# Gathering the half-array products of a hybrid decoder layer into common slots

## The chip, the cores and the metric

The kernel runs on one core of one Trainium2 chip. The metric is the device time of one execution in microseconds; before the change three runs took 1182.36 to 1182.70 us, median 1182.63.

## The reference

Two layers run one after the other on 256 tokens of width 1024, all in float32. Each layer is a mixer and a squared-ReLU MLP, with a layer norm after each. The mixer has one input projection and two branches: attention with 16 heads of 64 (the block of 256 tokens is the whole sequence, so it is plain causal attention), and a state-space branch with 32 heads of 64 in 8 groups, whose chunk is the whole sequence too.

```python
q, k, v, z, xbc, dt_raw, g_att, g_ssm = split(x @ w_in)
att   = softmax(causal(rope(q) @ rope(k).T / 8)) @ v                 # 16 heads
xs, bm, cm = split(silu(causal_conv(xbc)))
decay = exp(a_cs[l] - a_cs[s]) for s <= l                            # a_cs: running sum of dt * a
y     = (cm @ bm.T * decay * dt) @ xs + d_skip * xs                  # 32 heads, 8 groups
y     = rmsnorm(y * silu(z)) * ssm_norm_w
mix   = (sigmoid(g_att) * (att @ w_attn_proj) + sigmoid(g_ssm) * (y @ w_ssm_proj)) @ w_out
h     = LN(ALPHA * x + mix);  x = LN(ALPHA * h + relu(h @ w_up)**2 @ w_down)
```

## The kernel before

The kernel writes its order out by hand. The program is a row of slots of TensorE, 370 a layer; a slot is twelve products of 256 columns or six of 512. `plan_layer` hangs work on slot numbers: `slots[s]` holds the slot's own products of the large projections, and `at(s, step)` hangs any other step on a slot. The last loop of `trunk` goes through the slots and issues for each the weight splits that are due (`high_half`, L121, a cast on ACT; `low_half`, L129, a subtraction on DVE), then the steps in the order in which they were hung, then the weight loads (L115, SP's queue), then the slot's own products. Every engine works through its instructions in that order. `res(s)` returns the next slot that no other step has reserved for a temporary PSUM bank.

Every large product is made of three float32r products (high by high, high by low, low by high parts; L139 to L141 where 512 columns are streamed, L402 to L404 where 256 are). Weights are loaded in half units of 512 KB, eight slots before the cast, which is two slots before the subtraction, which is four slots before use.

Between the large products stand small ones in plain float32. For attention, a pair of heads p takes: `at_scores` (L631; rows of 64, one head in each half of the array, so 64x128; both temporary banks), `at_mask` on DVE (L639), `at_exp` on ACT (L646), `at_norm` on DVE (L651, L653), one `at_turn` a head (three transposes, L660, and a copy on ACT, L662), `at_av` (L674; 64 output columns a head, one head in each half of the array, so 128x64), and for every second p `at_out`. For the state space, a pair of heads p takes: `ss_load` (a broadcast DMA on SP's queue into `pb`), `ss_seg` on DVE (L720), `ss_exp` on ACT (L726), `ss_mask` on DVE (L734) and `ss_y` (L745, also 128x64). For every second p, g = p // 2, follow `ss_sum`, the gate, the squares and `ss_mean` (L784, a full-array float32 product), then the scaling and splitting. `at_av` and `ss_y` write to the two banks of tag `yav`.

Before, the scores of pair p start at the first free slot from AT0[p], which gives 95, 108, 115, 130, 137, 146, 155 and 166; the two `at_turn` follow from four slots after the first exponential, and `at_av` comes four slots after the second `at_turn`. `ss_y` of p comes at int(72 + 6.75 p) + 6. In slots 74 to 113 the large products are those of q, k and v with 512 columns; from 114 those of z and the gates with 256.

Of the kernel before, what the change touches and what calls it, by code (L numbers as in the profile page):

```python
# [11 lines left out]
F32 = mybir.dt.float32  # L12
# [6 lines left out]
S = 256  # L19
# [17 lines left out]
START = -10  # L37
AT0 = (95, 108, 109, 130, 134, 146, 155, 166)
SS0, SS_STRIDE = 72, 6.75


# [19 lines left out]
def trunk(ctx: ExitStack, tc: tile.TileContext, x, xT, pos, w, pch, hp, lnp, out):  # L61
# [7 lines left out]

    # The program is a row of slots of the tensor engine (about 6 products of 512 columns each).  # L70
    # Every slot first issues the weight loads and splits due in it, then the steps hung on it,
    # then its own products.
    slots = {}
    steps = defaultdict(list)
# [10 lines left out]
    def res(s):  # L85
        """the next slot in which nothing takes a bank for turning data."""
        s = int(s)
        while s in busy:
            s += 1
        busy.add(s)  # L90
        return s
# [12 lines left out]

# [1 line left out]
    raws = {}  # L106
# [35 lines left out]

# [1 line left out]
    def cols(base, L, h0, src, alloc, nk=KD, outer_from=None, quiet=False):  # L144
# [37 lines left out]

# [1 line left out]
    def rows(base, L, h0, k0, accs, src, outer=False):  # L184
# [24 lines left out]

# [1 line left out]
    ident = consts.tile([128, 128], F32, name="ident")  # L211
# [18 lines left out]

# [1 line left out]
    x_tok = consts.tile([128, 2, D], F32, name="x_tok")  # L232
# [22 lines left out]

# [1 line left out]
    cos2 = consts.tile([128, 2, 16], F32, name="cos2")  # L257
# [48 lines left out]

# [1 line left out]
    def new_T(name):  # L308
        return (u_tile(name + "h", F32R, (128, 4, S)), u_tile(name + "l", F32R, (128, 4, S)))

    def transpose_half(s, dst, src, t, j, name):
        """four 128-column blocks of one token tile."""
        tp = new_tmp(name).rearrange("p (k s) -> p k s", k=4)
        for k in range(4):
            nc.tensor.transpose(tp[:, k, :], src[:, k * 128:k * 128 + 128], ident)
        split_psum(s, dst[0][:, j:j + 4, t * 128:t * 128 + 128], dst[1][:, j:j + 4, t * 128:t * 128 + 128], tp)

    def transpose_pair(src, c, name):
        """two 128-column blocks of both token tiles."""
        tp = new_tmp(name).rearrange("p (k s) -> p k s", k=2)  # L320
        for k in range(2):
            for t in range(2):
                nc.tensor.transpose(tp[:, k, t * 128:t * 128 + 128],
                                    src[:, t, c + k * 128:c + k * 128 + 128], ident)
        return tp
# [3 lines left out]

# [1 line left out]
    class Norm:  # L331
# [47 lines left out]
    def plan_layer(L):  # L379
# [9 lines left out]

        at(B - 40 if L else START, load_params)  # L390
        xsrc = lambda k: (X[2 * L][0], X[2 * L][1], k)

        def gemm_ct(o, h, half, src=None, k0=None, nh=1):
            """a tile of 128 output columns, channel-major; four k-tiles of a half unit."""
            wh, wl = W[L, h]
            src = src or xsrc
            k0 = 4 * half if k0 is None else k0
            for i in range(4):
                k, c = k0 + i, (4 * half + i) * 128
                xh, xl, kk = src(k)  # L400
                a, b = wh[:, c:c + 128], wl[:, c:c + 128]
                nc.tensor.matmul(o, a, xh[:, kk, :], start=(k == 0), stop=False)  # L402
                nc.tensor.matmul(o, a, xl[:, kk, :], start=False, stop=False)  # L403
                nc.tensor.matmul(o, b, xh[:, kk, :], start=False, stop=(k == 8 * nh - 1))  # L404

# [1 line left out]
        def dt_slot(half):  # L407
# [72 lines left out]

# [1 line left out]
        XB = B + 10  # L482
# [56 lines left out]

# [1 line left out]
        T = {}  # L541
# [45 lines left out]

# [1 line left out]
        def ct_bank(base, h0, c0, c1, name, src, nh=1):  # L589
            """tiles c0..c1 of 128 output columns side by side in one bank."""  # L590
            g = {}

            def slot(c, half):
                if c == c0 and half == 0:
                    g["o"] = new_acc(f"acc_{name}{L}_{c}")
                o = g["o"][:, (c - c0) * S:(c - c0) * S + S]
                gemm_ct(o, h0 + nh * c + half // 2, half % 2, src, 4 * half, nh)

            for c in range(c0, c1):
                for half in range(2 * nh):  # L600
                    s = base + 2 * nh * c + half
                    if half % 2 == 0:
                        need(L, h0 + nh * c + half // 2, s)
                    slots[s] = (slot, c, half)
            return g

# [1 line left out]
        zs, ga, gs = {}, {}, {}  # L608
# [11 lines left out]

# [1 line left out]
        G = {}  # L622
# [61 lines left out]

        for p in range(8):
            s = B + AT0[p]
            while s in busy or s + 1 in busy:
                s += 1
            busy.update((s, s + 1))
            at(s, at_scores, p)  # L690
            for h in (2 * p, 2 * p + 1):
                at(s + 1, at_exp, h)
                at(s + 2, at_norm, h)
                s += 1
            s += 3
            for h in (2 * p, 2 * p + 1):
                s = res(s)
                at(s, at_turn, h)
                s += 1
            at(s + 3, at_av, p)  # L700
            if p % 2 == 1:
                at(s + 4, at_out, s + 4, p // 2)

# [1 line left out]
        E = {}  # L705
        yT = {}

        def ss_load(p):
            E["pb", p] = sb.tile([128, 2, S], F32, name=f"pb{L}_{p}", tag="pb", bufs=3)
            nc.sync.dma_start(out=E["pb", p].rearrange("p i s -> p (i s)"),  # L710
                              in_=P["csd"][2 * p:2 * p + 2, :].rearrange("h s -> (h s)").partition_broadcast(128))

        def ss_seg(p):
            pb = E.pop(("pb", p))
            e = sb.tile([128, 2, 384], F32, name=f"ev{L}_{p}", tag="e3", bufs=2)
            cst = P["cst"]
# [63 lines left out]
        def ss_mean(g):  # L780
            tp = new_tmp(f"sqp{L}{g}")
            sh = E.pop(("sh", g))
            for j in range(2):
                nc.tensor.matmul(tp[:, 0:S], ones, sh[:, j, :], start=(j == 0), stop=(j == 1))  # L784
            # every row of the product holds the sums; blocks of 32 columns turn them onto partitions
            r = sb.tile([128, S], F32, name=f"rs{L}{g}", tag="rs", bufs=1)
# [30 lines left out]
        free = 0  # L817
        for p in range(16):
            s = int(B + SS0 + SS_STRIDE * p)
            at(s - 12, ss_load, p)  # L820
            at(s - 1, ss_seg, p)
            at(s + 2, ss_exp, p)
            at(s + 3, ss_mask, p)
            at(s + 6, ss_y, p)
            if p % 2 == 1:
                g = p // 2
                at(s + 7, ss_sum, g)
                s = free = max(s + 8, B + 114 + 8 * (g // 2) + 10, free + 7)
                for i, step in ((-1, ss_gate), (1, ss_square), (2, ss_add), (3, ss_sq_high), (5, ss_sq_low)):
                    at(s + i, step, g)  # L830
                s = res(s + 8)
                at(s, ss_mean, g)
                at(s + 2, ss_rstd, g)
                at(s + 2, ss_scale, g)
                at(s + 3, ss_high, g)
                at(s + 5, ss_low, g)

# [1 line left out]
        mT, mb = {}, {}  # L839
# [30 lines left out]

# [1 line left out]
        at(B + 202, load_ln, gb1, L, 0)  # L872
# [23 lines left out]

# [1 line left out]
        M = B + 242  # L898
# [23 lines left out]

        # the other chunks channel-major: no turning needed
        ub = {}
# [116 lines left out]
def _cols(m, c0, n):  # L1041
    """n*512 columns -> for each 512, K/256 halves [128, 2 k, 512]."""
    kb = m.shape[0] // 256
# [4 lines left out]
def _rows(m):  # L1048
    """[K, 1024] -> K/128 halves [128, 1024]."""
    return m.reshape(-1, 128, D)  # L1050


def _tiles(m, starts):
    """tiles of 128 columns -> for each, K/1024 halves [128, 8 k, 128]."""
    out = [m[:, a:a + 128].reshape(-1, KD, 128, 128).transpose(0, 2, 1, 3).reshape(-1, 128, HALF) for a in starts]
    return np.concatenate(out)
# [62 lines left out]
```

## Time and profile before

| | |
|---|---|
| three runs | 1182.36 to 1182.70 us, median 1182.63 |
| span of the profiled execution, first to last instruction | 1179.1 us |
| PE (matmul) busy | 1160.1 us, 98% |
| PEld (weight load) busy | 1058.6 us, 90% |
| DVE busy | 865.3 us, 73% |
| ACT busy | 649.2 us, 55% |
| POOL busy | 51.1 us, 4% |
| chain that ended last | PE 96%, DVE 2%, DMA 1% |

The profile is that of one execution, and shows its span; the time of a run is counted around it and is some 3.5 us more. PE's matmuls are pipelined, so their durations overlap and the distance from one start to the next is what an instruction costs. The shapes after MATMUL are the rows and columns of the array that an instruction uses: 128*128 is the whole array.

### The profile page before, as it was taken

The page shows a single profiled execution, that of the slowest core. Times are in us where ns is not written, and L with a number is a line of the kernel's source. Part 1 is how long each engine was busy: PE and PEld are TensorE (multiplying, and loading weights), DVE is VectorE, ACT ScalarE, POOL GpSimd, SP SyncE. Part 2 cuts the span into 40 slices and gives each one's busy share as a digit, 9 for nine tenths or more (in the row PEclk, how much of TensorE's full clock was granted, in tenths as well). Part 3 has the DMA queues.
Part 4 walks back from the last instruction along what each step waited for, and adds up shares of the span by engine and source line. Part 5 has one row for each costly group of instructions (what it writes and reads, how often), then busy time and mean ns, then how long its engine had stood idle before and what let it go on. Part 6 is the DMA issues. An engine that isn't in the chain of part 4 may idle for free.

```text
span 1179.1 us, 20423 instructions
## 1 busy us (share of the span) xinstructions
PE 1160.1 (98%) x8160; PEld 1058.6 (90%) x8160; DVE 865.3 (73%) x1553; ACT 649.2 (55%) x927; POOL 51.1 (4%) x67
## 2 busy tenths in 40 slices
PE   6999999999999999999999999999999999999996
PEld 5999878999999889989889997789999998998995
DVE  4988977789866874564688888678997668556455
ACT  5665655788734363453456656568785343444341
POOL 1000000011110000000000000000110100000000
PEclk9999999999999999999999999999999999999999
DMA  9545554444466755556325455445534666555630
GB/s 348 193 143 180 188 176 150 166 144 144 147 208 218 249 183 187 190 201 246 133 99 216 158 191 187 162 143 171 161 134 172 220 218 207 204 179 183 210 125 36
DMA packets 61262, 211.37 MB, mean 179 GB/s; under 512 B 6992, under 2 KB 7344, under 8 KB 61168
## 3 DMA queue, kind: packets, MB, share of 16 engines
q1 hardware_dynamic: 59136, 204.04, 49.8%
q0 software_dynamic: 1744, 5.51, 1.5%
q8 instruction: 64, 1.05, 0.3%
q10 hardware_dynamic: 288, 0.52, 0.1%
q14 instruction: 30, 0.25, 0.1%
HBM read 208.93 MB, written 1.11 MB: 178 GB/s over the span
## 4 chain that ended last, share of the span: by engine, by line
PE 96%; DVE 2%; DMA 1%; SPq 0%; POOL 0%; issue 0%; POOLq 0%; ACT 0%
PE acc_x L402 5%; PE acc_x L403 5%; PE acc_x L404 5%; PE acc_d L140 5%; PE acc_d L139 5%; PE acc_d L141 5%; PE up L404 5%; PE up L403 5%; PE up L402 5%; PE acc_z L402 3%; PE acc_sp L403 3%; PE acc_sp L402 3%; PE acc_sp L404 3%; PE acc_z L403 3%; PE acc_z L404 3%; PE yp L745 2%
## 5 line engine op out<-in xcount | busy, mean ns | idle before, releaser
L129 DVE TENSOR_TENSOR wlo<-raw,whi 128x1024 fp32r<-128x1024 f32 (+1 forms) x371 | 443.7, 1216 | 28.7 <-ACT whi L121 12.7
L121 ACT CAST whi<-raw 128x1024 fp32r<-128x1024 f32 (+1 forms) x371 | 375.7, 1043 | 28.5 <-PE acc_ap L403 7.6
L500 DVE SCALAR_TENSOR_TENSOR cv<-acc_x,pc,cv 128x253 f32<-128x253 f32 (+2 forms) x192 | 92.3, 481 | 18.6 <-ACT cv L496 13.8
L909 DVE TENSOR_TENSOR rl<-rl 128x512 f32<-128x512 f32 x32 | 22.1, 691 | 110.6 <-ACT rl L905 110.5
L905 ACT ACTIVATE rl<-up 128x512 f32<-128x512 f32 x28 | 16.7, 598 | 154.1 <-PE up L404 134.3
L402 PE MATMUL acc_x<-x2h,whi 128*128 128x256 f32 x256 | 74.0, 289 | 0.0
L402 PE MATMUL acc_x<-x0h,whi 128*128 128x256 f32 x256 | 73.9, 289 | 0.0
L404 PE MATMUL acc_x<-x0h,wlo 128*128 128x256 f32 x256 | 72.4, 283 | 0.0
L404 PE MATMUL acc_x<-x2h,wlo 128*128 128x256 f32 x256 | 72.4, 283 | 0.0
L403 PE MATMUL acc_x<-x0l,whi 128*128 128x256 f32 x256 | 72.4, 283 | 0.0
L403 PE MATMUL acc_x<-x2l,whi 128*128 128x256 f32 x256 | 72.4, 283 | 0.0
L496 ACT ACTIVATE cv<-acc_x,pc 128x256 f32<-128x256 f32 x64 | 36.1, 564 | 62.3 <-PE acc_x L404 59.4
L402 PE MATMUL up<-x1h,whi 128*128 128x256 f32 x224 | 63.5, 284 | 0.0
L402 PE MATMUL up<-x3h,whi 128*128 128x256 f32 x224 | 63.5, 284 | 0.0
L404 PE MATMUL up<-x1h,wlo 128*128 128x256 f32 x224 | 63.4, 283 | 0.0
L404 PE MATMUL up<-x3h,wlo 128*128 128x256 f32 x224 | 63.4, 283 | 0.0
L403 PE MATMUL up<-x1l,whi 128*128 128x256 f32 x224 | 63.4, 283 | 0.0
L403 PE MATMUL up<-x3l,whi 128*128 128x256 f32 x224 | 63.4, 283 | 0.0
L328 POOL TENSOR_TENSOR rc<-rc,mhalf 128x8 f32<-128x8 f32 x16 | 28.2, 1765 | 624.4 <-DVE nm L651 496.3
L734 DVE SCALAR_TENSOR_TENSOR ev<-ev,dt,cb 128x256 f32<-128x256 f32 (+1 forms) x128 | 44.9, 413 | 9.8 <-ACT ev L726 9.8
L402 PEld LDWEIGHTS acc_x<-x0h,whi 128*128 128x128 f32 x256 | 49.0, 191 | 0.3 <-issue 0.2
L402 PEld LDWEIGHTS acc_x<-x2h,whi 128*128 128x128 f32 x256 | 49.0, 191 | 0.3 <-issue 0.2
(749 smaller groups left out, 3522.4 us busy)
## 6 DMA issues: line engine op xcount, KB each, us to landing
raw<-in_w_dram SPq DMA_DIRECT2D x369, 512.0 KB, 3.5
pb<-csd SPq DMA_DIRECT2D x32, 256.0 KB, 3.8
ln<-in_lnp_dram POOLq DMA_DIRECT2D x16, 256.0 KB, 4.8
x_tok<-in_x_dram POOLq DMA_DIRECT2D x1, 1024.0 KB, 10.2
xraw<-in_xT_dram SPq DMA_DIRECT2D x3, 256.0 KB, 7.2
raw<-in_w_dram SPq DMA_DIRECT2D x2, 256.0 KB, 3.7
out_dram<-x_tok SPq DMA_DIRECT2D x2, 256.0 KB, 2.0
out_dram<-x_tok ACTq DMA_DIRECT2D x2, 256.0 KB, 2.0
```

The costliest lines, as they stand in the source:

```text
L121: nc.scalar.copy(out=hi[:, c], in_=raws[key][:, c])
L129: nc.vector.tensor_tensor(out=lo[:, c], in0=raw[:, c], in1=W[key][:, c].bitcast(F32), op=OP.subtract)
L139: nc.tensor.matmul(o, xh, wh, start=first, stop=False)
L140: nc.tensor.matmul(o, xh, wl, start=False, stop=False)
L141: nc.tensor.matmul(o, xl, wh, start=False, stop=last)
L328: nc.gpsimd.tensor_tensor(out=dst, in0=src, in1=mhalf[:, 0:n], op=OP.pow)
L402: nc.tensor.matmul(o, a, xh[:, kk, :], start=(k == 0), stop=False)
L403: nc.tensor.matmul(o, a, xl[:, kk, :], start=False, stop=False)
L404: nc.tensor.matmul(o, b, xh[:, kk, :], start=False, stop=(k == 8 * nh - 1))
L496: nc.scalar.activation(c, o, AF.Identity, scale=pc[:, q + 3:q + 4], bias=pc[:, q + 4:q + 5])
L500: nc.vector.scalar_tensor_tensor(out=c[:, d:S], in0=o[:, 0:S - d], scalar=pc[:, q + j:q + j + 1], in1=c[:, d:S], op0=OP.mult, op1=OP.add)
L734: nc.vector.scalar_tensor_tensor(out=e[:, i, r], in0=e[:, i, r], scalar=dt[:, t, h:h + 1], in1=cb[:, r], op0=OP.mult, op1=OP.mult)
```

## The change

Two tables of slots replace AT0. `ss_y` of both p of a g is hung on one slot, SS_AT[g], which is the slot that the odd p had before. The scores go to the slots AT_S, `at_av` to the slots AT_V. The slots AT_S and the one behind each are reserved before anything else of the layer. The two `at_turn` of a pair are put in the first free slots from five before its AT_V. The loop over the state space comes before that over attention, so its steps are hung first. `ss_load` moves from 12 to 10 slots ahead, `pb` has two buffers instead of three, and `e3` three instead of two. Comments are taken out as well.

```diff
-AT0 = (95, 108, 109, 130, 134, 146, 155, 166)
 SS0, SS_STRIDE = 72, 6.75
+SS_AT = tuple(int(SS0 + SS_STRIDE * (2 * g + 1)) + 6 for g in range(8))
+AT_S = (98, 111, 118, 125, 132, 138, 145, 152)
+AT_V = (111, 125, 132, 138, 145, 152, 159, 165)
...
         at(B - 40 if L else START, load_params)
+        busy.update(B + v + i for v in AT_S for i in range(2))
...
-        for p in range(8):
-            s = B + AT0[p]
-            while s in busy or s + 1 in busy:
-                s += 1
-            busy.update((s, s + 1))
+        def at_pair(p):
+            s = B + AT_S[p]
             at(s, at_scores, p)
-            for h in (2 * p, 2 * p + 1):
-                at(s + 1, at_exp, h)
-                at(s + 2, at_norm, h)
-                s += 1
-            s += 3
-            for h in (2 * p, 2 * p + 1):
-                s = res(s)
-                at(s, at_turn, h)
-                s += 1
-            at(s + 3, at_av, p)
+            for i in range(2):
+                at(s + 1 + i, at_exp, 2 * p + i)
+                at(s + 2 + i, at_norm, 2 * p + i)
+            v = B + AT_V[p]
+            r = v - 5
+            for i in range(2):
+                r = res(r)
+                at(r, at_turn, 2 * p + i)
+                r += 1
+            assert r < v
+            at(v, at_av, p)
             if p % 2 == 1:
-                at(s + 4, at_out, s + 4, p // 2)
+                at(v + 1, at_out, v + 1, p // 2)
...
-            E["pb", p] = sb.tile([128, 2, S], F32, name=f"pb{L}_{p}", tag="pb", bufs=3)
+            E["pb", p] = sb.tile([128, 2, S], F32, name=f"pb{L}_{p}", tag="pb", bufs=2)
...
-            e = sb.tile([128, 2, 384], F32, name=f"ev{L}_{p}", tag="e3", bufs=2)
+            e = sb.tile([128, 2, 384], F32, name=f"ev{L}_{p}", tag="e3", bufs=3)
...
-        for p in range(16):
-            s = int(B + SS0 + SS_STRIDE * p)
-            at(s - 12, ss_load, p)
-            at(s - 1, ss_seg, p)
-            at(s + 2, ss_exp, p)
-            at(s + 3, ss_mask, p)
-            at(s + 6, ss_y, p)
-            if p % 2 == 1:
-                g = p // 2
-                at(s + 7, ss_sum, g)
-                s = free = max(s + 8, B + 114 + 8 * (g // 2) + 10, free + 7)
...
+        for g in range(8):
+            v = B + SS_AT[g]
+            for p in (2 * g, 2 * g + 1):
+                s = int(B + SS0 + SS_STRIDE * p)
+                at(s - 10, ss_load, p)
+                at(s - 1, ss_seg, p)
+                at(s + 2, ss_exp, p)
+                at(s + 3, ss_mask, p)
+                at(v, ss_y, p)
+            at(v + 1, ss_sum, g)
+            s = free = max(v + 2, B + 114 + 8 * (g // 2) + 10, free + 7)
...
+        for p in range(8):
+            at_pair(p)
```

## Rows read from the trace of the kernel before

**Rows 1.** The page: busy time of the engines, and the chain's shares.
```profile
PE 1160.1 (98%) x8160; PEld 1058.6 (90%) x8160; DVE 865.3 (73%) x1553; ACT 649.2 (55%) x927; POOL 51.1 (4%) x67
...
PE 96%; DVE 2%; DMA 1%; SPq 0%; POOL 0%; issue 0%; POOLq 0%; ACT 0%
```

**Rows 2.** All waits of PE; columns: us in total, times, longest us.
```profile
PE acc_q00a L139 <- ACT whi L121: 6.0, 2, 5.8
PE acc_q00a L140 <- DVE wlo L129: 3.1, 2, 2.3
PE lb0x L315 <- DVE x_tok L361: 0.7, 1, 0.7
```

**Rows 3.** Timeline of PE around a lone `ss_y`; columns: start us, duration us.
```profile
240.69 0.28 PE L404 MATMUL acc_z<-x0h,wlo 128*128 128x256 f32 x1
240.90 0.87 PE L745 MATMUL yp<-ev,xs 128*64 128x256 f32 x8
241.70 0.39 PE L402 MATMUL acc_z<-x0h,whi 128*128 128x256 f32 x1
241.92 0.28 PE L403 MATMUL acc_z<-x0l,whi 128*128 128x256 f32 x1
242.04 0.28 PE L404 MATMUL acc_z<-x0h,wlo 128*128 128x256 f32 x1
```

**Rows 4.** Timeline of PE around an `at_av` and an `ss_y` in one slot.
```profile
291.41 0.28 PE L404 MATMUL acc_gs<-x0h,wlo 128*128 128x256 f32 x1
291.62 0.87 PE L674 MATMUL av<-pts,v 128*64 128x256 f32 x8
292.32 0.82 PE L745 MATMUL yp<-ev,xs 128*64 128x256 f32 x8
...
293.29 0.28 PE L403 MATMUL acc_gs<-x0l,whi 128*128 128x256 f32 x1
```

**Rows 5.** Timeline of PE around a group of scores.
```profile
256.03 0.28 PE L404 MATMUL acc_z<-x0h,wlo 128*128 128x256 f32 x1
256.24 0.93 PE L631 MATMUL sp<-kT,qT 64*128 64x128 f32 x8
...
257.32 0.28 PE L403 MATMUL acc_ga<-x0l,whi 128*128 128x256 f32 x1
```

**Rows 6.** Timeline of PE: an `ss_mean` with an `ss_y` behind it, and alone.
```profile
229.14 0.28 PE L404 MATMUL acc_z<-x0h,wlo 128*128 128x256 f32 x1
229.26 0.40 PE L784 MATMUL sqp<-sh,ones 128*128 128x256 f32 x2
229.59 0.87 PE L745 MATMUL yp<-ev,xs 128*64 128x256 f32 x8
...
230.61 0.28 PE L403 MATMUL acc_z<-x0l,whi 128*128 128x256 f32 x1
...
243.11 0.28 PE L404 MATMUL acc_z<-x0h,wlo 128*128 128x256 f32 x1
243.23 0.40 PE L784 MATMUL sqp<-sh,ones 128*128 128x256 f32 x2
...
243.59 0.29 PE L403 MATMUL acc_z<-x0l,whi 128*128 128x256 f32 x1
```

**Rows 7.** Timelines of DVE and PE: the first `ss_mask` and the first `ss_y`.
```profile
130.47 1.40 DVE L734 SCALAR_TENSOR_TENSOR ev<-ev,dt,cb 128x256 f32<-128x256 f32 x4
...
132.91 0.87 PE L745 MATMUL yp<-ev,xs 128*64 128x256 f32 x8
```

**Rows 8.** Timelines of ACT and PE: layer 0's last copy and `at_av`.
```profile
307.58 0.47 ACT L662 COPY pts<-pt 128x384 f32<-128x384 f32 x1
...
312.26 0.87 PE L674 MATMUL av<-pts,v 128*64 128x256 f32 x8
```

**Rows 9.** Busy by stretch; columns: PE, PEld, DVE, ACT, POOL, granted clock, DMA.
```profile
276.00:292.00 16.00, 16.00 (x136) 15.03 (x136) 15.79 (x36) 12.56 (x25) 1.74 (x1) 1.00 0.43 149
```

**Rows 10.** The page: the pb loads; columns: KB each, us to landing.
```profile
pb<-csd SPq DMA_DIRECT2D x32, 256.0 KB, 3.8
```

More of the change, by code (lines that the diff above doesn't have):

```diff
@@ L817, in plan_layer @@
         free = 0
-        for p in range(16):
-            s = int(B + SS0 + SS_STRIDE * p)
-            at(s - 12, ss_load, p)
-            at(s - 1, ss_seg, p)
-            at(s + 2, ss_exp, p)
-            at(s + 3, ss_mask, p)
-            at(s + 6, ss_y, p)
-            if p % 2 == 1:
-                g = p // 2
-                at(s + 7, ss_sum, g)
-                s = free = max(s + 8, B + 114 + 8 * (g // 2) + 10, free + 7)
[L829 to L836, printed above, removed]
+        for g in range(8):
[9 more added lines that the diff above has]
+            s = free = max(v + 2, B + 114 + 8 * (g // 2) + 10, free + 7)
+            for i, step in ((-1, ss_gate), (1, ss_square), (2, ss_add), (3, ss_sq_high), (5, ss_sq_low)):
+                at(s + i, step, g)
+            s = res(s + 8)
+            at(s, ss_mean, g)
+            at(s + 2, ss_rstd, g)
+            at(s + 2, ss_scale, g)
+            at(s + 3, ss_high, g)
+            at(s + 5, ss_low, g)
+        for p in range(8):
+            at_pair(p)
         mT, mb = {}, {}
```

## The prediction

> **What bounds the kernel now.** The first view is the page's table of busy time with its chain: PE is busy 98% of the span and carries 96% of the chain that ended last [rows 1]. The second is the list of what PE waited for: three rows, 9.8 us, two at the start of the program and one at the layer boundary, none at a product of attention or state space [rows 2]. So in the stretch that the change touches PE is never short of an operand, and the time there is what PE takes to work through its row of instructions. What the other engines do matters only if it comes to hold PE up. The third view, the timeline of PE, therefore carries the prediction: it shows how long PE stays away from its full-array products for each small product.
>
> **How a small product is priced.** In the stream of float32r products the starts stand 0.12 us apart (241.92 to 242.04) [rows 3]. For a lone group of eight instructions of `ss_y` I take the start of the last full product before it and of the second one after it, since that second one is late too: 240.69 to 241.92 is 1.23 us, and two ordinary steps of 0.12 would be 0.24, so the group costs 0.99 us [rows 3]. Where an `at_av` and an `ss_y` already share a slot, the two together take 291.41 to 293.29, 1.88 us, less 0.24, which is 1.64 [rows 4]. The second group adds 0.65 us, 0.34 less than it costs alone. Those 0.34 us are the two changes between full-array products and products of 128x64: after the last full product the first small one starts 0.21 us later instead of 0.12; on the way back 241.70 to 241.92 is 0.22 instead of 0.12 [rows 3]. A group of scores (64x128) costs 256.03 to 257.32, 1.29 less 0.24, 1.05 us [rows 5]. It holds as many instructions with as many columns as an `at_av` (half of 128, half of 256), so its body is near 0.65 too, and its two changes cost 0.40, about 0.20 each.
>
> **The change, part by part.**
>
> *State space and attention output in common slots.* Before, a layer has `ss_y` in 16 slots (78 to 179, every 6 or 7) and `at_av` in 8 (105, 118, 125, 140, 147, 156, 165, 176). Four are common (105, 118, 125, 165), so there are 20 excursions to the 128x64 shape. After, both `ss_y` of a g go to SS_AT = 84, 98, 111, 125, 138, 152, 165, 179, and `at_av` to 111, 125, 132, 138, 145, 152, 159, 165: 11 different slots. Nine excursions a layer disappear. Two or three groups stand together then; a pair of `ss_y` or a row of three is not in the trace. The bounds are 0 (the join is not one, as between `ss_mean` and `ss_y`, below) and 0.34 from the join of `at_av` with `ss_y`; the shape is the same in all three, so I take 0.34: 9 x 0.34 = 3.06 us a layer.
>
> *Scores in front of the return.* Before, the 8 scores stand in slots of their own. After, seven of the AT_S (98, 111, 125, 132, 138, 145, 152) are among the eleven slots, and 118 stands alone: 12 slots in all instead of 28. The loop over g hangs its steps first, then `at_pair` does, so in such a slot PE has `ss_y`, `at_av`, scores. This order, 128x64 straight to 64x128, is nowhere in the trace. What joining different kinds does in the nearest row: a lone `ss_mean` (full array, float32) costs 243.11 to 243.59 less 0.24, 0.24 us; with an `ss_y` behind it the two take 229.14 to 230.61 less 0.24, 1.23 us, which is 0.24 + 0.99: nothing gained [rows 6]. There the number of changes of shape stays two. Here it falls from four to three, so one of about 0.20 us should go: 7 x 0.20 = 1.40 us a layer. The bounds are 0 (as in rows 6) and 0.40 (both shapes run into each other without any pause). I take 0.20, because every change between two shapes that the rows do show pays its pause.
>
> The Trainium skill, TensorEngine Tiling (Array Packing), Key Properties, says that a change of the tiling mode drains the engine, while a change of tile within a mode does not. The pauses in rows 3 and 5 and the missing one in rows 4 agree; no run here shows the step from one half-array mode to the other. By that rule the sum below stands. The same list says that tiles operate independently and may load and multiply in parallel; read across the modes, the result would be that of the first rival.
>
> *Sum.* (3.06 + 1.40) x 2 layers = 8.9 us. The profiled execution has a span of 1179.1 us [rows 1], 3.5 below the median of the runs shown, 1182.63; what lies around the span is not touched. The span goes to 1170.2, the time to 1173.7 us.
>
> **What I cost at nothing, and what covers it.**
>
> *Masks before `ss_y`.* DVE's `ss_mask` is three slots ahead of its product. The first of the program ends at 131.87 (130.47 + 1.40) and the product starts at 132.91, a lead of 1.04 us [rows 7]. The odd p keep their slots and now stand behind the even one (0.65 us more lead); the even ones wait 6 or 7 slots longer. The third `e3` buffer pays for that: `ss_seg` of p+2 falls in the slot of the two products, and DVE can run it ahead of them.
>
> *Transposed probabilities before `at_av`.* Before, `at_av` is 4 slots behind its second `at_turn`; after it is 4, 4, 4, 2, 3, 3, 3, 3. A slot of twelve products is 12 x 0.12 = 1.44 us. The last `at_av` of layer 0 has its ACT copy done at 308.05 (307.58 + 0.47) and starts at 312.26, a lead of 4.2 us [rows 8]. Two slots less would leave 1.3; but at slot 138 two `ss_y` groups stand ahead of it and give 1.3 back. At slot 159 nothing stands ahead: 4.2 - 1.4 = 2.8 us remain, less what ACT is later there, since the exponentials of p = 7 now come just before those copies (152 to 155 instead of 166 to 168). If this cover goes, PE waits the difference, once or twice a layer.
>
> *DVE's queue.* `at_mask` now stands behind up to three groups of products, so DVE may reach it early and stand still, with the norm and later weight splits (L129) behind it. The splits are hung four slots (5.8 us) ahead of use. But DVE has little to spare: 15.79 of 16 us in one such stretch [rows 9]. Its work per slot is as before; attention is pressed from slots 95 to 177 into 98 to 166. This is the cover that may fail: the third rival.
>
> *The pb loads.* 16 a layer, moved from 12 to 10 slots ahead, in two buffers instead of three. They stand in SP's queue among the weight loads. The buffer of p-2 was read 4.5 slots before the new issue, so SP should not stop there, and 3.8 us to landing [rows 10] fits into the nine slots (13 us) until `ss_seg`. Cover gone, SP's weight loads would queue behind it; they have eight slots of their own.
>
> *Banks and moved transposes.* Keeping AT_S and the slot behind it free moves one k turn (111 to 113) and the means by up to two slots; their number stays. yav banks alternate between y and av; each is emptied one slot after its last product, 6 slots or more before its next use. Scores take both tmp banks and the next user comes two slots later.
>
> **The rivals.**
>
> 1. *The scores join for nothing.* If products of 64x128 start while those of 128x64 still run, each join gives 0.40: 2.8 us more, 1170.9 us. Nothing in rows 3 to 6 shows two shapes overlapping.
> 2. *The scores join gains nothing,* as `ss_mean` with `ss_y`: only the 3.06 x 2 remain, 1176.5 us. For it: the only mixed join in the trace behaves so. Against it: the count of changes there is unchanged.
> 3. *PE waits at the gathered slots (slower).* DVE, and ACT behind it, come late with the masks and copies that PE now wants at one point, and everything of PE queues behind the half-array products. It decides from 8.9 us over 22 slots, 0.4 us of waiting each; at 0.6 us each the time is 1173.7 + 13.2 = 1186.9 us. For it: DVE's 15.79 of 16 us, and the lead of 1.04 us. Against it: rows 2 show no wait although those stretches exist already, and most leads grow.
>
> That the slots are not gathered is no rival: the numbers above are sums of the constants.
>
> **How the numbers follow.** Forecast 70%, rival 1 8%, rival 2 10%, rival 3 12%. Of the last, half ends slower than before by over 0.2% (2.4 us, about what a measurement of this kernel can tell from no change), half within that. So faster 0.88, same 0.06, slower 0.06. The range 1170.8 to 1176.8 reaches over both bounds of the scores' join and leaves out rival 3.
>
> **What would show it.** On PE's timeline of after: eleven stretches of 128x64 products a layer, the second and third group in one adding 0.65 us; the first score 0.2 us behind the last `ss_y` or `at_av`, and a score group adding 0.85 us to its slot (0.65 by rival 1, 1.05 by rival 2). PE's list of waits stays at three rows near 10 us. A new row there with L745, L674 or L631, released by DVE or ACT, is rival 3. The granted clock is 1.00 in the stretch of rows 9; a lower one beside the longest gathered stretches (about 3 us of half-array products, where 1.65 us was the most) would make the prediction wrong in a way that I have not priced.

## The result and the profile after

The kernel after takes 1172.95 us (median of four runs, 1171.82 to 1173.77) against 1182.49 before, a ratio of 0.992 with a 95% interval of 0.9908 to 0.9932: 9.5 us faster, where 1173.7 us and 8.9 us were forecast. The profiled execution has a span of 1170.6 us, 8.5 less. The page's first lines answer to [rows 1]: DVE and ACT are busy as long as before within 1.5 us, PE 9.2 us less, and the chain that ended last is again PE's to 96%.

```profile
span 1170.6 us, 20414 instructions
PE 1150.9 (98%) x8160; PEld 1058.4 (90%) x8160; DVE 864.3 (74%) x1553; ACT 650.7 (56%) x927; POOL 54.9 (5%) x67
```

All waits of PE, as in [rows 2] (total, times, longest): none is at a small product. The fourth row is new, but stands at the program's first products.

```profile
PE acc_q00a L143 <- ACT whi L125: 6.3, 2, 6.1
PE acc_q00a L144 <- DVE wlo L133: 3.3, 2, 2.5
PE lb0x L319 <- DVE x_tok L365: 0.8, 1, 0.8
PE acc_q00a L143 <- ACT x0h L254: 0.2, 1, 0.2
```

The timeline of PE at slot 138 (`ss_y` is L748, `at_av` L679, the scores L636), and a group of scores by itself at slot 118:

```profile
238.47 0.28 PE L409 MATMUL acc_z<-x0h,wlo 128*128 128x256 f32 x1
238.68 1.52 PE L748 MATMUL yp<-ev,xs 128*64 128x256 f32 x16
240.03 0.82 PE L679 MATMUL av<-pts,v 128*64 128x256 f32 x8
240.78 0.93 PE L636 MATMUL sp<-kT,qT 64*128 64x128 f32 x8
...
241.86 0.28 PE L408 MATMUL acc_z<-x0l,whi 128*128 128x256 f32 x1
...
201.49 0.28 PE L409 MATMUL acc_z<-x0h,wlo 128*128 128x256 f32 x1
201.70 0.93 PE L636 MATMUL sp<-kT,qT 64*128 64x128 f32 x8
...
202.78 0.28 PE L408 MATMUL acc_z<-x0l,whi 128*128 128x256 f32 x1
```

By the reckoning of [rows 3], the stretch of four groups costs 238.47 to 241.86 less two steps of 0.12, 3.15 us: 0.99 + 0.65 + 0.65 + 0.86. The lone group of scores costs 1.05, so the join saves 0.19. Reckoned so over both layers, with steps of 0.227 us where 512 columns are streamed, all stretches with products of attention and state space cost 61.9 us before (without the transposes and means that shared a slot with some) and 52.9 after, 9.0 less.

There is a second reading, which needs no reckoning of single stretches. PE works through the same 5760 large products in every kernel here, so I compare when it starts the same one: the 121st, behind the first ten slots, which no edit touches, and the second one behind the last `ss_y` of layer 1. Before:

```profile
35.15 0.28 PE L402 MATMUL acc_x<-x0h,whi 128*128 128x256 f32 x1
...
898.69 0.28 PE L403 MATMUL acc_ap<-attT11l,whi 128*128 128x256 f32 x1
```

After:

```profile
35.89 0.28 PE L407 MATMUL acc_x<-x0h,whi 128*128 128x256 f32 x1
...
890.21 0.28 PE L408 MATMUL acc_ap<-attT11l,whi 128*128 128x256 f32 x1
```

From the one to the other PE took 863.54 us before and takes 854.32 after, 9.2 us less (4.57 in layer 0, 4.65 in layer 1), as much as its busy time fell by. Below I call this PE's way. It leaves out what differs from one execution to the next at the program's start. It is longer than the 9.0 because in the stretch of 512 columns more than two products behind a detour come late (behind a lone `ss_y` they stand 0.34 and twice 0.24 us apart instead of 0.23).

The granted clock is 1.00, which is 2.4 GHz, the higher of its two levels, from 276 to 292 us as in [rows 9], and in the whole of 130 to 330 and 700 to 910 us, so the longer rows of half-array products did not lower it.

### The profile page after: what moved, and what is told of

The parts are those of the page before. It is cut to its first block, busy times and chain, and to the rows that moved or that the text cites. A ratio compares the mean times of both kernels' runs of the same rounds, so it can differ in the third digit from the quotient of the medians.

```text
span 1170.6 us, 20414 instructions
## 1 busy us (share of the span) xinstructions
PE 1150.9 (98%) x8160; PEld 1058.4 (90%) x8160; DVE 864.3 (74%) x1553; ACT 650.7 (56%) x927; POOL 54.9 (5%) x67
## 3 DMA queue, kind: packets, MB, share of 16 engines
q8 instruction: 64, 1.05, 0.4%
## 4 chain that ended last, share of the span: by engine, by line
PE 96%; DVE 2%; DMA 1%; SPq 0%; POOL 0%; issue 0%; POOLq 0%; ACT 0%
PE acc_x L407 5%; PE acc_x L409 5%; PE acc_x L408 5%; PE acc_d L143 5%; PE acc_d L145 5%; PE acc_d L144 5%; PE up L409 5%; PE up L408 5%; PE up L407 5%; PE acc_z L407 3%; PE acc_sp L409 3%; PE acc_sp L408 3%; PE acc_sp L407 3%; PE acc_z L408 3%; PE acc_z L409 3%; PE yp L748 2%
## 5 line engine op out<-in xcount | busy, mean ns | idle before, releaser
L332 POOL TENSOR_TENSOR rc<-rc,mhalf 128x8 f32<-128x8 f32 x16 | 32.0, 2002 | 612.1 <-DVE nm L656 445.0
L408 PEld LDWEIGHTS acc_x<-x0l,whi 128*128 128x128 f32 x256 | 49.1, 192 | 0.0
```

The costliest lines, as they stand in the source:

```text
L332: nc.gpsimd.tensor_tensor(out=dst, in0=src, in1=mhalf[:, 0:n], op=OP.pow)
```

## The experiments

Three theories: S, PE pays for each change of array shape; I, it pays for each interruption of its float32r stream, whatever the shape; Q, the gain is freed queues. Times stand beside runs of the kernel before on the same chip (medians of 1181.1 to 1182.2 us), so ratios compare better than times; all changes are to the kernel after. Most differences are smaller than what a few runs can tell, and there PE's way decides: in two profiles of the kernel after it agrees within 0.03 us. A change of number format alone is not what PE pays for: an `ss_mean`, float32 on the whole array, costs its two steps of 0.12 and no more [rows 6].

**Half of the change.** The old attention loop and AT0 are put back, and the slots AT_S are no longer reserved. A part of the edit:

```diff
-        for p in range(8):
-            at_pair(p)
+        for p in range(8):
+            s = B + AT0[p]
...
```

> Only the state space half of the change: both ss_y of a g share a slot (with the new buffers of pb and e3), attention stays in its slots of before. Theory S (PE pays for each change of array shape): 20 excursions to the 128x64 shape a layer become 14, two of the six removed ones in the stretch of 512 columns (0.39 us each by the trace of before), four in that of 256 (0.34): 2.14 us a layer, 4.3 in all, 1178.2 us against 1182.5 of before. Theory I (each interruption of the float32r stream costs the same, whatever its shape; 9.2 us over the 32 slots that the whole change removes, 0.29 each): 12 slots, 3.5 us, 1179.0. Theory Q (the gain is freed queues, not PE's own work, and needs attention moved too): nothing, 1182.5.

Measured 1177.95 us against 1182.22, ratio 0.9964 (0.9951 to 0.9977). Theory Q falls. S and I lie too close here to be told apart by the time. PE's way can: it is 4.95 us longer than in the kernel after, so 4.3 shorter than before, which is S's 4.3 and not I's 3.5.

**Scores a slot behind.**

```diff
-        busy.update(B + v + i for v in AT_S for i in range(2))
+        busy.update(B + v + 1 + i for v in AT_S for i in range(2))
...
-            s = B + AT_S[p]
+            s = B + AT_S[p] + 1
```

> The kernel after, but every group of scores is put one slot behind its stretch of 128x64 products, so that seven a layer stand alone again. Theory S: a group of scores costs 1.05 us alone and 0.86 joined, so 7 x 2 x 0.19 = 2.7 us slower than after, 1175.6 us; the stretches left behind cost 2.29 (three groups) and 0.99 (one). Theory I: 14 interruptions more at 0.29, 4.1 us, 1177.0. Theory Q: nothing, 1172.9.

Measured 1175.21 us (ratio 0.9945, 0.9928 to 0.9962), which leaves room for S and for I. PE's way grows by 2.6 us, where S has 2.7 and I 4.1. On PE's timeline, the stretch that was 3.15 us falls into one of 2.29 (238.46 to 240.99 less 0.24) and one of 1.05 (242.18 to 243.47 less 0.24):

```profile
238.46 0.28 PE L409 MATMUL acc_z<-x0h,wlo 128*128 128x256 f32 x1
238.67 1.52 PE L748 MATMUL yp<-ev,xs 128*64 128x256 f32 x16
240.02 0.82 PE L679 MATMUL av<-pts,v 128*64 128x256 f32 x8
...
240.99 0.28 PE L408 MATMUL acc_z<-x0l,whi 128*128 128x256 f32 x1
...
242.18 0.28 PE L409 MATMUL acc_z<-x0h,wlo 128*128 128x256 f32 x1
242.39 0.93 PE L636 MATMUL sp<-kT,qT 64*128 64x128 f32 x8
...
243.47 0.28 PE L408 MATMUL acc_z<-x0l,whi 128*128 128x256 f32 x1
```

**Scores between the other two.** `at_first`, taken out of `at_pair`, hangs the scores, exponentials and norms; `at_pair` keeps the transposes, `at_av` and `at_out`. Its loop stands ahead of `at_pair`'s:

```diff
+        for p in range(8):
+            at_first(p)
         for p in range(8):
             at_pair(p)
```

> The kernel after, but in each common slot the scores stand between ss_y and at_av, so PE goes 128x64, 64x128, 128x64. Theory S: one change of shape more in the four slots a layer that hold all three kinds, into 128x64 at 0.15 us: the stretch of four groups grows from 3.15 to 3.30 us, 1.2 us over both layers, 1174.1 us. Where only at_av and scores share a slot, the number of changes stays and the stretch too (1.85). Theory I: as many slots as after, so nothing, 3.15 us and 1172.9.

Measured 1174.08 us (two runs; the ratio, 0.9932, 0.9911 to 0.9953, does not tell it from the kernel after). The timeline of PE does: at the same slot 240.25 to 243.79 less 0.24 is 3.30 us with the same 32 instructions, and PE's way grows by 1.4 us, where S has 1.2 and I nothing. The number of slots did not change; the number of changes of shape did. That tells S from I.

```profile
240.25 0.28 PE L409 MATMUL acc_z<-x0h,wlo 128*128 128x256 f32 x1
240.46 1.52 PE L750 MATMUL yp<-ev,xs 128*64 128x256 f32 x16
241.91 0.93 PE L636 MATMUL sp<-kT,qT 64*128 64x128 f32 x8
242.76 0.87 PE L679 MATMUL av<-pts,v 128*64 128x256 f32 x8
...
243.79 0.28 PE L408 MATMUL acc_z<-x0l,whi 128*128 128x256 f32 x1
```

**Scores first.** The same loop, ahead of the loop over g.

> The kernel after, but in each common slot the scores stand first, so PE goes 64x128, then 128x64. Theory S: as many changes as after, so the stretch of four groups stays within 0.05 us of 3.15, and the time at 1172.9. Theory I: the same. What it tells: whether the saving hangs on the order of the two shapes, and whether scores that come 0.65 to 2 us sooner give DVE its work sooner, so that the shortest leads of masks and copies before PE's products (0.17 and 0.57 us in the kernel after) grow.

Measured 1172.78 us, and 3.15 us for the stretch: the order of the two shapes is indifferent; PE's way is the same within 0.05 us. The two shortest leads became 0.35 and 0.75 us.

**Both transposes of a pair in one slot.**

```diff
-            r = v - 5
+            r = res(v - 5)
+            assert r < v
             for i in range(2):
-                r = res(r)
                 at(r, at_turn, 2 * p + i)
-                r += 1
-            assert r < v
```

> The kernel after, but both at_turn of a pair of heads share one slot: 16 interruptions of the stream fewer over both layers, all of them in the full-array shape. Theory S: a join of groups of the same full-array shape removes no change of shape, so the pair costs 2 x 0.33 = 0.66 us and the time stays 1172.9. Theory I (0.29 us for each interruption): 4.6 us faster, 1168.3.

Measured 1174.47 us (ratio 0.9939, 0.9926 to 0.9953): not faster. A pair costs 258.38 to 259.27 less 0.24, 0.65 us. A lone one, here from the further step below, costs 276.65 to 277.22 less 0.24, 0.33. So a pair is twice a lone one; theory I falls here.

```profile
258.38 0.28 PE L409 MATMUL acc_ga<-x0h,wlo 128*128 128x256 f32 x1
258.50 0.82 PE L665 MATMUL pt<-ident,pe 128*128 128x128 f32 x6
...
259.27 0.28 PE L408 MATMUL acc_ga<-x0l,whi 128*128 128x256 f32 x1
...
276.65 0.28 PE L409 MATMUL acc_ga<-x0h,wlo 128*128 128x256 f32 x1
276.77 0.49 PE L665 MATMUL pt<-ident,pe 128*128 128x128 f32 x3
...
277.22 0.28 PE L408 MATMUL acc_ga<-x0l,whi 128*128 128x256 f32 x1
```

What made it slower is a new row in PE's waits. The two transposes now want both temporary banks at once: at 283.17 us the second head's start only at 284.56, when ACT's copy of the first head's has ended (284.51), while the mean of slot 160 still holds the other bank (DVE reads it from 284.92). PE's way grows by 2.4 us, more than the list books:

```profile
PE pt L665 <- ACT pts L667: 1.8, 2, 0.9
```

**`at_av` of p = 6 a slot earlier**, for the third rival:

```diff
-AT_V = (111, 125, 132, 138, 145, 152, 159, 165)
+AT_V = (111, 125, 132, 138, 145, 152, 158, 165)
```

> The kernel after, but at_av of p = 6 one slot earlier (158 instead of 159), its two at_turn where they were. In the kernel after the copies that it reads are done 0.57 us before it starts; a slot is 1.43 us. If PE takes what it wants when it is there and otherwise stands still (the third rival of the prediction, at one place), PE waits 0.86 us there in each layer, 1.7 us in all, 1174.6 us, and a row for av released by ACT's copy (pts) appears in PE's waits. If the lead hides more than it shows, nothing: 1172.9.

Measured 1174.15 us (two runs). PE starts with the head whose copy is there, stops, and goes on at 278.53: the excursion costs 277.43 to 279.55 less 0.24, 1.88 us instead of 0.99. In the list of waits the new row for av holds only part of it, 0.5 us over both layers; the starts show the whole, 0.89 a layer, and PE's way grows by 1.8 us.

```profile
277.43 0.28 PE L409 MATMUL acc_ga<-x0h,wlo 128*128 128x256 f32 x1
277.64 0.65 PE L679 MATMUL av<-pts,v 128*64 128x256 f32 x2
278.53 0.86 PE L679 MATMUL av<-pts,v 128*64 128x256 f32 x6 [0.25 <-ACT pts L667]
...
279.55 0.28 PE L408 MATMUL acc_ga<-x0l,whi 128*128 128x256 f32 x1
```

**The buffers of before**: three of `pb`, two of `e3`.

> The kernel after with the buffers of before: three of pb, two of e3. ss_seg of p+2 then has to wait for ss_y of p, which stands in the same slot. Theory S: PE's own work is the same, so 1172.9 us unless PE waits. DVE stands still at ss_seg until the even product is through, at most the time by which it runs ahead of PE; the shortest lead before an ss_y is 0.17 us, so I expect PE's waits to stay below 1 us in all, 1172.9 to 1173.9. If the third buffer is what makes the gathering possible (third rival of the prediction), PE waits in most of the eight common slots a layer: 1178 or more.

Measured 1172.71 us (two runs). DVE does stand still at `ss_seg` for PE's `ss_y` (6.7 us in three waits in the stretch of layer 0), but PE has no new wait, and its way is the same within 0.03 us. The third `e3` buffer is worth nothing here.

**A step further, ten slots a layer.**

```diff
-U_BUFS = 31
+U_BUFS = 29
-SS_AT = tuple(int(SS0 + SS_STRIDE * (2 * g + 1)) + 6 for g in range(8))
+SS_AT = tuple(int(SS0 + SS_STRIDE * (2 * max(g, 1) + 1)) + 6 for g in range(8))
-AT_V = (111, 125, 132, 138, 145, 152, 159, 165)
+AT_V = (111, 125, 132, 138, 145, 152, 165, 165)
...
-            r = v - 5
+            r = v - 5 - 2 * (p == 6)
```

(and four buffers of `pt` and `e3`).

> A step further in the same direction: ss_y of p = 0 and 1 move from slot 84 to 98 beside those of 2 and 3, and at_av of p = 6 from 159 to 165 beside that of 7, so ten slots a layer instead of twelve. This takes four buffers each of e3 and pt, paid with two fewer of the 4 KB buffers of tag u (29), which mostly hold weights. Theory S: two excursions a layer less, one at 0.39 and one at 0.34 us, 1.46 us in all, 1171.5 us. Against it: weight loads are issued later with fewer buffers, and if a split comes late PE waits; nothing of that shows up to now, so I expect under 0.5 us of it.

Measured 1172.13 us, not to be told from the kernel after. The products themselves came out 1.4 us shorter, as reckoned, but PE's way did not (0.15 us longer): PE waited, a new row being `ss_mean` for ACT's copy (0.8 us in two waits). So the two transposes of p = 6 went back (`r = v - 11` for p = 6), once with the scores behind, once with the scores first, beside new runs of the kernel after on that chip:

> The kernel after itself, on the same chip as the two that follow, for the comparison: 1172.9 us by its first runs.

> The step further again (ten slots a layer), with the two at_turn of p = 6 back in 155 and 156, where the kernel after has them. In the first try they stood in 158 and 159, and the mean in 160 waited twice 0.4 us for the bank that ACT's late copy of the second one held; that and late banks elsewhere gave back 1.3 of the 1.4 us that the products saved. If that bank wait is what gave it back, the row sqp released by ACT's copy goes from PE's waits, and the time is 1.4 us under that of the kernel after, 1171.5 us. If the two fewer buffers of tag u are what costs, it stays where it was, level with the kernel after.

> The same with the scores first in every common slot. Theory S: as many changes of shape, so the same 1171.5 us; the leads of masks before the products are longer (0.35 against 0.17 us at the shortest in the kernels with twelve slots), so if any wait is left in the one before, it is smaller here.

Measured 1173.0, 1173.35 and 1173.18 us: no gain, where I expected 1.4 us. In the first of the two further kernels the mean's wait for ACT's copy is gone, as expected, but its second product now waits for DVE (`sh` is done at 281.91): the two take 281.61 to 282.31 less 0.24, 0.46 instead of 0.24. And the transposes at 162 wait for a bank: 285.28 to 286.37 less 0.24, 0.85 instead of 0.33:

```profile
281.61 0.28 PE L409 MATMUL acc_ga<-x0h,wlo 128*128 128x256 f32 x1
281.72 0.63 PE L787 MATMUL sqp<-sh,ones 128*128 128x256 f32 x2
...
282.31 0.28 PE L408 MATMUL acc_ga<-x0l,whi 128*128 128x256 f32 x1
...
285.28 0.28 PE L409 MATMUL acc_ga<-x0h,wlo 128*128 128x256 f32 x1
285.87 0.55 PE L665 MATMUL pt<-ident,pe 128*128 128x128 f32 x3 [0.31 <-ACT pts L667]
...
286.37 0.28 PE L408 MATMUL acc_gs<-x0l,whi 128*128 128x256 f32 x1
```

That is 0.74 us, against the 0.72 (0.38 and 0.34) that the layer saves. Without the excursion at 159 PE comes to slots 160 to 162 sooner, and DVE, which shows no gap from 277.8 to 287 us, and ACT, which waits for DVE there (0.92 us before 283.74), don't. With the scores first the wait for that bank is no smaller (0.7 us booked over both layers against 0.6), against what I expected, though PE's way is 0.17 us shorter. The fewer buffers of tag u show in no wait. The last kernel leaves that place alone and keeps only the other half (slot 84 into 98, `e3` 4, tag u 30):

> Only the half of the further step that lies far from ACT's busy stretch: ss_y of p = 0 and 1 in slot 98 beside those of 2 and 3 (four buffers of e3, 30 of tag u), at_av of p = 6 back in 159. In the two kernels with both halves the stretch up to slot 110 came out 0.38 us shorter in layer 0, and what the other half saved was given back at slots 160 to 162, where PE waited for a bank that ACT empties. If that is so, no wait is new here and both layers keep their 0.38 us: 0.76 us under the kernel after, 1172.2 us, which is less than the runs can tell apart, so the timeline of PE is to show it. If a shorter stretch ahead always turns into waits at 160 to 162, the gain is gone again by slot 170.

Measured 1171.13 us (ratio to before 0.9919, 0.9906 to 0.9933). It is the lowest median of all, but on the chip where the kernel before has its lowest too (1181.1), and the runs can't tell it from the kernel after (0.992). PE's timeline can: the common stretch costs 163.27 to 167.53 less two steps of 0.227, 3.81 us, where the kernel after has 1.65 and 2.51 in two slots; no new wait appears, and PE's lead on the kernel after grows by 0.37 us in each layer and stays.

```profile
163.27 0.39 PE L145 MATMUL acc_q01b<-whi,x0l 128*128 128x512 f32 x1
163.59 2.82 PE L748 MATMUL yp<-ev,xs 128*64 128x256 f32 x32
166.34 0.93 PE L636 MATMUL sp<-kT,qT 64*128 64x128 f32 x8
...
167.53 0.40 PE L144 MATMUL acc_k01a<-wlo,x0h 128*128 128x512 f32 x1
```

## Why the prediction was right

*The join of 128x64 groups.* Forecast 0.65 us for a second or third group; measured 0.65. Of the nine joins a layer, three are in the stretch of 512 columns. There a lone group costs 1.01 us and two together 1.65 up to the second product behind them, a saving of 0.37, and 0.39 with the later products that come late, too. The sum, which took 0.34 for all, missed 0.3 us of it over both layers.

*The scores.* Forecast 0.85 us joined, measured 0.86, between the bounds of 0.65 and 1.05; rivals 1 and 2 are out. The 0.20 for the change that goes was chosen between two bounds, with no row of before for this step, and it held. That it is one change of shape that went is shown by the kernel with the scores in the middle, where one came back and cost 0.15. By the rule on modes in the Trainium skill, TensorEngine Tiling (Array Packing), Key Properties, the sum was to stand, and the trace agrees: read start by start, the first score follows the last `at_av` product after 0.20 us, where a group of the same shape follows at the same place after 0.11.

*What a change of shape does.* PE's weight loads show it; the prediction makes no use of them. Here they are for the kernel before, around [rows 4]:

```profile
291.29 0.19 PEld L404 LDWEIGHTS acc_gs<-x0h,wlo 128*128 128x128 f32 x1
291.62 0.63 PEld L674 LDWEIGHTS av<-pts,v 128*64 128x64 f32 x8
292.21 0.68 PEld L745 LDWEIGHTS yp<-ev,xs 128*64 128x64 f32 x8
293.07 0.19 PEld L402 LDWEIGHTS acc_gs<-x0h,whi 128*128 128x128 f32 x1 [0.17 <-issue]
```

As long as the shape stays, loads run ahead of their products (between full-array ones by 0.12 us at the median): at 291.29 for the full product of 291.41, at 292.21 for the first `ss_y` product of 292.32, though that one begins a new group. Where the shape changes, the load starts only with its product: 291.62 for `at_av`, 293.07 on the way back. From 130 to 330 us this is so at each of the 56 changes of before and of the 31 of after (within 0.002 us). The 25 that went are the nine detours of two changes and the seven joins of scores that the prediction counted. By PE's way a change that went was worth 4.57 / 25, 0.18 us. That the late load is the whole of the price is not shown.

*The sum.* The stretches give 9.0 us and PE's way 9.2, against 8.9. The span fell by 8.5 only because in this execution the program's first products came late: PE's waits sum to 10.6 us against 9.8 in [rows 2], and after ten slots, which the change does not touch, PE is 0.74 us behind. This is not the change's: a second profile of the same kernel is another 0.6 us later there, and the kernel with the scores a slot behind, whose first ten slots are the same, stands at 35.17 us, where the kernel before has 35.15. The 3.5 us between the span and the time of a run, which the text ahead of the prediction takes for what lies around the span, are not that either: wherever both are on record for one run, they differ by 1.7 to 2.1 us, so the profiled execution of before was one of the shorter ones. The forecast does not depend on it, since it takes the same 8.9 us off both. That the time came to within 0.8 us of it is in part luck: single runs of one kernel differ by 2 us.

*The covers.* No wait appeared, but less cover was left than I reckoned; here the prediction's reasons were wrong in two places, and it came out right since neither cover was used up. ACT's second copy for p = 6 ends at 279.09 and `at_av` starts at 279.66: 0.57 us, where I had 2.8 less what ACT is late, a lateness that I left without a number. And I wrote that the odd p gain 0.65 us of lead: in slot 165 the mask of p = 13 ends at 290.70, after the even product has started at 290.16. Its own product, 0.7 us on, finds it 0.17 us old; before, its lead was 2.9.

```profile
278.62 0.47 ACT L667 COPY pts<-pt 128x384 f32<-128x384 f32 x1
...
279.66 0.87 PE L679 MATMUL av<-pts,v 128*64 128x256 f32 x8
...
289.30 1.40 DVE L737 SCALAR_TENSOR_TENSOR ev<-ev,dt,cb 128x256 f32<-128x256 f32 x4
...
290.16 1.52 PE L748 MATMUL yp<-ev,xs 128*64 128x256 f32 x16
```

So the third rival was nearer than its 12% looked: at slot 159 one slot less was enough for a wait, as the kernel with that edit shows.

## What to carry to other kernels

Where PE is never short of an operand, count its changes of array shape. Here a detour into half-array products and back costs two of them (0.34 us for 128x64); joining two detours of one shape saves both, joining two of different shapes saves one (0.19), while joining transposes, small products on the full array, saves nothing. Find the price from start to start in the trace, up to the second product after the detour, and check it against when PE starts the same large product further on. Then look at the leads of what the joined products read: once a lead is used up, a shorter PE stretch only becomes a wait, as with ten slots a layer.

## What was not expected

The changes of shape do not all cost the same. This is an estimate, and takes the price to depend only on the shape that PE goes to: back to the full array 0.19 us (1.05 less 0.86), into 128x64 0.15 (3.30 less 3.15, and also 0.34 less 0.19), into 64x128 0.21 (0.40 less 0.19, with 0.65 for the scores themselves). And the list of waits can understate a wait: 0.25 us booked, 0.89 by the starts. PE had started two of the eight products before it stopped, and their bars run on to 278.29, so only the gap from there to 278.53 is booked.
